# Hybrid attention and retention layer: what goes through which pass of the input projection, how squares and input sums are made, and the order of the work

## The chip, the cores and the metric

The kernel runs on one core of one Trainium2 chip. The metric is the time of one execution on the device in microseconds; lower is better. A profiled execution of the kernel before is at hand: every instruction of the five engines (TensorE = PE, VectorE = DVE, ScalarE = ACT, GpSimd = POOL, SyncE = SP, which issues most transfers) and every transfer, with start and duration.

## What is computed

One decoder layer on 4096 rows of width 1024, float32. An RMS norm is followed by one input projection whose columns feed two groups: eight heads of rotary, dilated window attention and four heads of retention. Both are gated, concatenated, projected back and added to the input; a last RMS norm closes.

```python
def reference(x, norm_gain, w_in, ret_gn_gain, w_out, final_gain):
    for layer in range(DEPTH):
        h = rms_norm(x, norm_gain[layer])
        x = x + hybrid_mixer(h, w_in[layer], ret_gn_gain[layer], w_out[layer])
    return rms_norm(x, final_gain)

def hybrid_mixer(h, w_in, ret_gn_gain, w_out):
    proj = h @ w_in
    qa, ka, va, ga, qr, kr, vr, gr = jnp.split(proj, cuts, axis=-1)
    attn = merge_heads(dilated_attention(qa, ka, va))   # heads split; rotary q, k; branches (128,1), (512,4), (2048,16)
    ret = merge_heads(retention(qr, kr, vr))            # rotated q, k; chunks of 128; group norm
    ret = ret * ret_gn_gain
    mixed = jnp.concatenate([jax.nn.silu(ga) * attn, jax.nn.silu(gr) * ret], axis=-1)
    return mixed @ w_out
```

What matters here is `proj` for the attention's q, k, v and the retention's q, k ("r" below), with the rotation of q, k and r.

## The kernel before

The program has three stages. Stage 1 (`phase1`) makes q, k, r and v and writes them to device memory. Stage 2 (`phase2`) reads them back and computes attention and retention; stage 3 makes the gates and the output projection. Only stage 1 is touched.

**Passes, blocks, steps.** Stage 1 goes twice over the 4096 positions, each time in 8 blocks of 512 (`BLK`), so in 16 blocks `q` = 0 to 15; `q < NBLK` (8) is pass 0. A pass computes two groups of 512 output columns, `bank` 0 and 1. Before, pass 0 made q (bank 0) and k (bank 1), pass 1 made r (bank 0) and v (bank 1). The weights of a pass lie in SBUF; those of pass 1 are made while the last block of pass 0 and the first of pass 1 run.

**Seven products in place of eight.** A block's product of a 2 x 2 arrangement is made with seven smaller products of sums (Strassen's scheme in Winograd's form). The input of a block is split into four tiles of 128 x 1024 elements: `a1`, `a2` are the first and second 256 positions of the upper half of the contraction, `b1`, `b2` those of the lower. P1 takes a1, P2 b1, P3 b2, and P5, P6, P7, P4 take sums of them (`sum_t`, n = 1 to 4, on GpSimd, into tiles `d` of their own). Each product accumulates in one of three kinds of PSUM bank, `x` (3 buffers), `y` (2) or `z` (2), by the table `SUMS`. `snapshot` copies a bank's state to a tile `m` on ScalarE, `join` adds a bank to such a tile on VectorE.

**Precision.** Each factor is split into a high part (ScalarE, `AF.Copy` to the rounded type) and a low part (the rest, on VectorE or GpSimd), and each product is three products of parts: 24 matrix products of 128 x 128 by 256 columns for one product and bank. That is one *step*; a block has `STEPS` = 14 steps, two for each entry of `PRODUCTS`, bank 0 and then bank 1.

**What sets the order.** The order is written by hand and kept on every engine. `at(step, function, ...)` enters work for a step, and the loop at the end of the function goes through the steps, emits the step's product and then what is entered for it. `s` is the first step of a block, so an entry at `s + 11` stands in the block's twelfth step and one at `s + 17` in the fourth step of the next block. On each engine instructions run in this order; SP issues the transfers in this order, and one that has to wait holds back those behind it.

**Around a block.** `load_x` brings the input in two halves of 1 MB. In pass 0 `square` squares it on ScalarE in eight pieces and adds them up on GpSimd; `root` reduces over the partitions with four products, takes the power on GpSimd and forms a diagonal, `along_free` spreads it over the partitions with a product and stores it for pass 1, which loads it in `load_rb`. `load_tables` loads cosines and sines of the block into one buffer `tab`, `scale_tables` multiplies them by the norm's factors on GpSimd. `last_sum` calls `rotate` (six VectorE operations on 512 columns) for q, k and r in two halves of 256 positions each, at steps 11, 13, 15 and 17, and stores them: q and k split into high and low part, r as it is. In pass 1 `store_values` stores v three times in the orders that the three branches want, twelve transfers for each half. Buffers: `rawp` 3 inputs of 1 MB, `dp` 2 sums, `op` 2 for `o` (outputs of `rotate`) and 2 for `hl` (split outputs and v), `mp` 7, one for each tag of `tp`.

**Towards stage 2.** Entries at the end of the last block load stage 2's weights (`w2_load`), the first k (`first_k`), input (`first_chunk`) and the first half of q (`first_q`, two steps before the last product).

Of the kernel before, what the change touches and what calls it, by code (L numbers as in the profile page):

```python
# [8 lines left out]
F32 = mybir.dt.float32  # L9
# [16 lines left out]
D = 1024  # L26
# [92 lines left out]
PRODUCTS = ("P1", "P2", "P6", "P5", "P7", "P3", "P4")  # L119
# [19 lines left out]
def phase1(tc, io, dr, right, ahead):  # L139
# [5 lines left out]
    with ExitStack() as ctx:  # L145
# [33 lines left out]
        def pieces(p, tags, n):  # L179
            def get(dt):  # L180
# [23 lines left out]
                "P1": ("wh0", "q00"),  # L204
                "P2": ("wh1", "h0"),
                "P6": ("q01", "p40"),
                "P7": ("wl0", "wl1"),
                "P3": ("h1", "q10"),
# [3 lines left out]
                "P2": ("wh0", "wl0"),  # L212
                "P6": ("wh1", "wl1"),
                "P5": ("h0", "h1"),
                "P7": ("q00", "q10"),
                "P3": ("q01", "q11"),
# [4 lines left out]
        def load_w(ps, dst, part, k):  # L221

            rows = io["w1"][k * 128 : (k + 1) * 128, :]
            if ps == 0:
                src = rows[:, 0:1024].rearrange("k (u t c) -> k t u c", t=2, c=128)[:, part]
                nc.sync.dma_start(dst.rearrange("k (u c) -> k u c", c=128), src)
            else:
                src = rows[:, 1024:1536].rearrange("k (u t c) -> k t u c", t=2, c=128)[:, part]
                nc.sync.dma_start(dst[:, 0:256].rearrange("k (u c) -> k u c", c=128), src)
                nc.sync.dma_start(dst[:, 256:512], rows[:, 1536 + 256 * part : 1792 + 256 * part])  # L230
# [41 lines left out]
        xraw, xsum, xs = {}, {}, {}  # L272
        NB2 = 2 * NBLK

        def load_x(q, part, one=None):

            b = q % NBLK
            if (q, part) not in xraw:
                xraw[q, part] = rawp.tile([128, 4, BLK], F32, tag="x", name="xt1")
            cols = slice(b * BLK, (b + 1) * BLK)  # L280
            if one is None:
                nc.sync.dma_start(xraw[q, part], by_blocks(io["xT"])[:, 4 * part : 4 * part + 4, cols])
            else:
                k, hs = one
                cols = slice(b * BLK + hs.start, b * BLK + hs.stop)
                nc.sync.dma_start(xraw[q, part][:, k, hs], io["xT"][(4 * part + k) * 128 : (4 * part + k + 1) * 128, cols])

        H1, H2 = slice(0, HALF), slice(HALF, BLK)

        def sum_t(q, n):  # L290
            a, b = xraw[q, 0], xraw[q, 1]
            if n == 4:
                t = xsum[q, 2]
            else:
                t = dp.tile([128, 4, HALF], F32, tag="d", name="d1")
            x, y, o = {
                1: (a[:, :, H2], a[:, :, H1], ALU.subtract),
                2: (xsum.get((q, 1)), b[:, :, H2], ALU.subtract),
                3: (b[:, :, H2], a[:, :, H2], ALU.subtract),
                4: (b[:, :, H1], t, ALU.add),  # L300
            }[n]
            nc.gpsimd.tensor_tensor(t, x, y, o)  # L302
            xsum[q, n] = t

        def source(q, prod):
            a, b = xraw[q, 0], xraw[q, 1]
            if prod == "P1":
                return a[:, :, H1]
            if prod == "P2":
                return b[:, :, H1]  # L310
            if prod == "P3":
                return b[:, :, H2]
            return xsum[q, {"P5": 1, "P6": 2, "P7": 3, "P4": 4}[prod]]

        def split_x(q, prod, engine=None, each=False):
            t = xs[q, prod] = hp.tile([128, 2, 4, HALF], F32R, tag="h", name="h1")
            src = source(q, prod)
            for ks in [slice(k, k + 1) for k in range(4)] if each else [slice(0, 4)]:
                nc.scalar.activation(t[:, 0, ks, :], src[:, ks, :], AF.Copy)  # L319
                (engine or nc.vector).tensor_tensor(t[:, 1, ks, :], src[:, ks, :], f32(t[:, 0, ks, :]), ALU.subtract)  # L320

        sums = {}

        def square(q, j):

            sq = tp.tile([128, BLK], F32, tag="sq" if j else "acc", name="sq1")
            nc.scalar.activation(sq, xraw[q, j // 4][:, j % 4, :], AF.Square)
            if j:
                nc.gpsimd.tensor_tensor(sums[q], sums[q], sq, ALU.add)
            else:  # L330
                sums[q] = sq

        def root(b):

            ss = pss.tile([128, 512], F32, tag="ss", name="ss1")
            acc = sums.pop(b)
            for i in range(4):
                nc.tensor.matmul(
                    ss[:, i : i + 1],
                    acc[:, i * 128 : (i + 1) * 128],  # L340
                    ones[:, 0:1],
                    start=i == 0,
                    stop=i == 3,
                    skip_group_check=True,
                )
            v = sm.tile([128, 4], F32, tag="v", name="v1")
            nc.vector.tensor_scalar(v, ss[:, 0:4], 1.0 / D, NORM_EPS, ALU.mult, ALU.add)
            cols = rs[:, 4 * b : 4 * b + 4]
            nc.gpsimd.tensor_tensor(cols, v, mhalf, ALU.pow)
            diag = tp.tile([128, 4, 128], F32, tag="sq", name="diag1")  # L350
            nc.gpsimd.tensor_tensor(
                diag, ident.unsqueeze(1).broadcast_to([128, 4, 128]), cols.unsqueeze(2).broadcast_to([128, 4, 128]), ALU.mult
            )
            return diag

        def along_free(b, diag):

            ps = pss.tile([128, BLK], F32, tag="ss", name="rb1")
            nc.tensor.matmul(ps, ones, diag.rearrange("p c i -> p (c i)"), start=True, stop=True)
            rb = tp.tile([128, BLK], F32, tag="rb", name="rb1")  # L360
            nc.scalar.activation(rb, ps, AF.Copy)
            nc.sync.dma_start(dr["rs"][b].rearrange("(o i) p -> o (i p)", o=1), rb[0:1, :])
            return rb
# [7 lines left out]
        def load_tables(q):  # L371
            b, n = q % NBLK, "AR"[q // NBLK]
            tab = tabs[q] = tp.tile([128, 2, BLK], F32, tag="tab", name="tab1")
            for i, nm in enumerate((f"cos{n}", f"sin{n}")):
                nc.sync.dma_start(tab[:, i, :], io[nm][:, b * BLK : (b + 1) * BLK].unsqueeze(0).broadcast_to([4, 32, BLK]))

        def scale_tables(q):
            for i in range(2):
                nc.gpsimd.tensor_tensor(tabs[q][:, i, :], tabs[q][:, i, :], rbs[q], ALU.mult)
# [65 lines left out]
        def value_tile(q, half):  # L445
            if (q, half) not in vfs:
                vfs[q, half] = op.tile([128, 2, 512], F32, tag="hl", name="vo1")
            return vfs[q, half]
# [1333 lines left out]
```

## Time and profile before

| | us |
|---|---|
| median of 3 runs | 2683.66 (2680.44 to 2690.35) |
| the profiled execution | 2687.92 |
| its span, first to last instruction | 2685.8 |

| engine | busy us | share of the span |
|---|---|---|
| TensorE, products | 2347.0 | 87% |
| VectorE | 1734.0 | 65% |
| ScalarE | 1117.9 | 42% |
| GpSimd | 991.5 | 37% |

The shares are means over three stages with different limits. In the page's row of TensorE by fortieths of the span (67 us each) the first fifteen, stage 1, hold 3 to 7 tenths, and nearly all later ones 9.

### The profile page before, as it was taken

To read this page: it belongs to the slowest core of one execution; us is meant where nothing else is said; L and a number is where in the kernel's file an instruction comes from. 1 tells how busy PE (TensorE), PEld (TensorE's weight loads), DVE (VectorE), ACT (ScalarE), POOL (GpSimd) and SP (SyncE) were. 2 spreads that over 40 slices of the span, in tenths; PEclk is the share of its full clock that TensorE was granted. 3 is DMA by queue.
4 is the path that set the end of the run, shared out by engine and by line. 5 is a ranking of instruction groups with operands and counts; after the bars stand their busy time and mean duration, and the time that the engine had idled before them with its cause. 6 is when DMAs were issued, how large, how long until landed. Compare 5 with 4: busy or idle time off the path is not lost.

```text
span 2685.8 us, 47219 instructions
## 1 busy us (share of the span) xinstructions
PE 2347.0 (87%) x16872; PEld 2116.3 (79%) x16872; DVE 1734.0 (65%) x4129; ACT 1117.9 (42%) x3039; POOL 991.5 (37%) x860
## 2 busy tenths in 40 slices
PE   3677777667788756999999999999889999999998
PEld 3677777667788754888888888888678999989997
DVE  5676667685434434777878878888676565656563
ACT  3433333342122112666666666666632232323231
POOL 4544554543232333443534435344622121212110
PEclk7888888879888877999999999999999999999999
DMA  4233333533444356586576765855577656566563
GB/s 132 89 110 121 107 102 103 165 122 109 130 134 153 111 161 178 139 183 149 134 182 143 172 156 139 191 125 133 171 180 169 152 154 155 153 154 152 159 141 103
DMA packets 450074, 383.90 MB, mean 143 GB/s; under 512 B 193224, under 2 KB 397128, under 8 KB 444720
## 3 DMA queue, kind: packets, MB, share of 16 engines
q1 hardware_dynamic: 449024, 379.06, 53.6%
q8 instruction: 133, 2.18, 0.3%
q0 software_dynamic: 528, 1.58, 0.2%
q14 instruction: 101, 0.83, 0.1%
q10 hardware_dynamic: 288, 0.26, 0.0%
HBM read 262.15 MB, written 118.64 MB: 142 GB/s over the span
## 4 chain that ended last, share of the span: by engine, by line
PE 57%; DMA 14%; DVE 13%; SPq 4%; issue 4%; ACT 4%; POOL 4%; DVEq 0%; ACTq 0%; POOLq 0%
PE S L987 8%; PE O L1057 6%; PE T L1024 5%; PE po L48 4%; PE po L50 4%; PE po L49 4%; PE g L49 4%; PE g L50 4%; PE g L48 4%; PE x L407 3%; DMA tab<-in_cosR_dram 3%; PE V L48 2%; DMA tab<-in_sinA_dram 2%; PE V L50 2%; DMA dr_v<-vo 2%
## 5 line engine op out<-in xcount | busy, mean ns | idle before, releaser
L1008 DVE CUSTOM_DVE_ANT_0 S<-S,mask 128x256 f32<-128x256 f32 (+1 forms) x768 | 308.4, 402 | 181.9 <-PE S L987 147.8
L1015 ACT ACTIVATE P<-S,nm 128x256 f32<-128x256 f32 (+1 forms) x768 | 337.3, 449 | 50.7 <-DVE nm L1008 47.5
L50 PE MATMUL g<-h,wg 128*128 128x256 f32 x1024 | 290.2, 283 | 0.0
L407 PE MATMUL x<-h,w1q 128*128 128x256 f32 x832 | 181.1, 316 | 68.3 <-ACT m L428 63.2
L1571 POOL TENSOR_TENSOR rs<-v,mhalf 128x1 f32<-128x1 f32 x32 | 17.5, 547 | 551.9 <-DVE v L1569 534.2
L1024 PE MATMUL T<-ident,P 128*128 128x128 f32 x1368 | 214.1, 274 | 0.0
L407 PEld LDWEIGHTS x<-h,w1q 128*128 128x128 f32 x832 | 150.6, 222 | 71.7 <-ACT m L428 65.6
L49 PE MATMUL po<-wo,m 128*128 128x512 f32 x512 | 200.5, 392 | 0.0
L50 PEld LDWEIGHTS g<-h,wg 128*128 128x128 f32 x1024 | 196.6, 192 | 0.0
L1057 PE MATMUL O<-pt,v 128*64 128x128 f32 (+1 forms) x1968 | 196.4, 326 | 0.0
L987 PE MATMUL S<-kk,qc 128*128 128x256 f32 x1024 | 187.1, 306 | 7.7 <-issue 2.8
L755 POOL TENSOR_TENSOR hc<-hr,hc 128x512 fp32r<-128x512 f32 x64 | 85.4, 1335 | 273.5 <-ACT hc L754 187.6
L48 PE MATMUL po<-wohi,m 128*128 128x512 f32 x448 | 178.9, 399 | 7.1 <-ACT m L40 6.7
L987 PEld LDWEIGHTS S<-kk,qc 128*128 128x128 f32 x1024 | 149.5, 190 | 36.5 <-issue 18.6
L50 PE MATMUL po<-wohi,m 128*128 128x512 f32 x448 | 177.4, 397 | 0.2 <-DVE m L41 0.2
L319 ACT ACTIVATE h<-d 128x1024 fp32r<-128x1024 f32 x64 | 67.7, 1058 | 253.6 <-POOL d L302 147.8
L1057 PEld LDWEIGHTS O<-pt,v 128*64 128x64 f32 x1968 | 121.4, 137 | 60.8 <-issue 32.1
L1024 PEld LDWEIGHTS T<-ident,P 128*128 128x128 f32 x1368 | 164.5, 142 | 0.2 <-ACT wg0hi L87 0.2
L1015 ACT ACTIVATION_READ_ACCUMULATOR P<-S,nm 128x1 f32 x768 | 157.4, 205 | 0.0
L407 PE MATMUL x<-h,w1wh 128*128 128x256 f32 x384 | 89.7, 333 | 74.0 <-DVE o L484 60.5
L1510 ACT ACTIVATE e<-g 128x256 f32<-128x256 f32 x128 | 48.2, 379 | 250.9 <-PE g L50 232.1
L320 DVE TENSOR_TENSOR h<-d,h 128x1024 fp32r<-128x1024 f32 x46 | 70.2, 1526 | 125.1 <-ACT h L319 121.8
(273 smaller groups left out, 6966.8 us busy)
## 6 DMA issues: line engine op xcount, KB each, us to landing
hr<-in_xT_dram SPq DMA_DIRECT2D x64, 512.0 KB
q<-dr_q SPq DMA_DIRECT2D x128, 256.0 KB
xt<-in_xT_dram SPq DMA_DIRECT2D x30, 1024.0 KB
wb<-dr_w SPq DMA_DIRECT2D x128, 192.0 KB
o<-dr_o SPq DMA_DIRECT2D x192, 128.0 KB
v<-dr_v SPq DMA_DIRECT2D x94, 256.0 KB
dr_q<-hl SPq DMA_DIRECT2D x64, 256.0 KB
dr_k<-hl SPq DMA_DIRECT2D x64, 256.0 KB
```

The source lines that it names most:

```text
L48: nc.tensor.matmul(out, wh, xh, start=first and i == 0, stop=False)
L49: nc.tensor.matmul(out, wh, xl, start=False, stop=False)
L50: nc.tensor.matmul(out, wl, xh, start=False, stop=last and i == n - 1)
L319: nc.scalar.activation(t[:, 0, ks, :], src[:, ks, :], AF.Copy)
L320: (engine or nc.vector).tensor_tensor(t[:, 1, ks, :], src[:, ks, :], f32(t[:, 0, ks, :]), ALU.subtract)
L407: nc.tensor.matmul(o, l, r, start=first and j == 0, stop=last and j == 2, skip_group_check=True)
L755: nc.gpsimd.tensor_tensor(hc[:, :, 1, :], src, hc[:, :, 0, :].bitcast(F32), ALU.subtract)
L987: nc.tensor.matmul(s[:, j * 256 : (j + 1) * 256], qq[h, t, half][:, off : off + 128] if br == 0 else it["q"][:, t, i, :], rhs, start=(j == ...
L1008: nc.vector.tensor_tensor_reduce(sv, sv, mask[:, it["br"], c0:256], 1.0, BIG, ALU.add, ALU.min, accum_out=nm[:, col : col + 1])
L1015: nc.scalar.activation(it["P", i // 2][:, i % 2, c0:256], sv, AF.Exp, bias=nm[:, col : col + 1], scale=-1.0, accum_out=den[:, col : col + 1])
L1024: nc.tensor.transpose(t[:, j * 128 : (j + 1) * 128], it["P", bank][:, j // 2, j % 2 * 128 : j % 2 * 128 + 128], ident)
L1057: nc.tensor.matmul(o[64 * bank : 64 * bank + 64, c0 : c0 + 128 * m], vt[h, br, idx // 8][:, idx % 8, :], it["pt"][:, a : a + m, :].rearran ...
```

## The change

Nine things are changed in `phase1`, all of them together:

1. Pass 0 makes k (bank 0) and r (bank 1), pass 1 makes q (bank 0) and v (bank 1). So pass 0 rotates and stores k and r, pass 1 rotates and stores q and stores v.
2. The products come in the order P1, P5, P6, P3, P7, P2, P4, with other homes for their weights.
3. The input of a block comes in four tiles of 512 KB (`xq`, 6 buffers), one for each of a1, a2, b1, b2. `sum_t` runs on VectorE and writes over one of these tiles (a1 three times, a2 once); the tiles `d` are gone.
4. All low parts of the input are made on VectorE; high and low parts are entered at steps of their own (`hi_x`, `lo_x`).
5. The squares are summed along the rows of x as it lies in memory: `load_n` brings 128 rows of 1024 (512 KB) into one buffer `xn`, `square` squares them on ScalarE with a sum along the row. GpSimd's sums and the four products in `root` are gone; its diagonal takes the buffer `xn` too.
6. Tables come in halves with a buffer for each (k's or q's rotation, r's; first and second half), entered 8 to 11 steps ahead of their rotation; GpSimd scales cosine and sine of a half in one operation.
7. Rotation, high part, low part and store are entered at steps of their own. r's rotated output, the split outputs and v share 3 buffers `hl`.
8. In `store_values` the eight transfers for branch 1 are issued by GpSimd in place of SP.
9. Weights and squares of block 0, the weights of pass 1 and the loads for stage 2 are entered at other places; `first_q` comes four steps before the end.

```diff
-PRODUCTS = ("P1", "P2", "P6", "P5", "P7", "P3", "P4")
+PRODUCTS = ("P1", "P5", "P6", "P3", "P7", "P2", "P4")
...
-        rawp = pool("p1x", 3)
+        rawp = pool("p1x", 6)
         hp = pool("p1h", 3)
-        dp = pool("p1d", 2)
...
         op = pool("p1o", 2)
+        hlp = pool("p1hl", 3)
...
+        def sum_t(q, n, engine=None):
+
+            a1, a2, b1, b2 = (xq[q, i, j] for i in range(2) for j in range(2))
+            out, x, y, o = {
+                1: (a1, a2, a1, ALU.subtract),
+                2: (a1, a1, b2, ALU.subtract),
+                3: (a2, b2, a2, ALU.subtract),
+                4: (a1, b1, a1, ALU.add),
             }[n]
-            nc.gpsimd.tensor_tensor(t, x, y, o)
-            xsum[q, n] = t
+            (engine or nc.vector).tensor_tensor(out, x, y, o)
...
+        def load_n(q, i):
+            xn[q, i] = tp.tile([128, D], F32, tag="xn", name="xn1")
+            n = 4 * q + i
+            nc.sync.dma_start(xn[q, i], io["x"][n * 128 : (n + 1) * 128, :])
+
+        def square(q, i):
+
+            if i == 0:
+                sums[q] = sm.tile([128, 4], F32, tag="ssq", name="ssq1")
+            t = xn.pop((q, i))
+            nc.scalar.activation(t, t, AF.Square, accum_out=sums[q][:, i : i + 1])
...
+            tab = tabs[q, n, half] = tp.tile([128, 2, HALF], F32, tag=f"tab{n}{half}", name="tab1")
...
-                    nc.sync.dma_start(dr["v"][1, r0 : r0 + 32].rearrange("(a l) e -> l a e", a=4), vf[r:128:4, u, :])
+                    nc.gpsimd.dma_start(dr["v"][1, r0 : r0 + 32].rearrange("(a l) e -> l a e", a=4), vf[r:128:4, u, :])
...
+            if bank:
+                t = hlp.tile([128, 2, BLK], F32, tag="hl", name="or1")
+                o1, o2 = t[:, 0, :], t[:, 1, :]
+            else:
+                o1, o2 = (op.tile([128, BLK], F32, tag="o", name=f"o{i}_1") for i in "12")
...
+                for n, (part, half) in zip((12, 10, 8, 5), ((0, 0), (0, 1), (1, 1), (1, 0))):
+                    at(s - n, load_x, q, part, half)
+                at(s - 4, hi_x, q, "P1")
+                at(s - 3, lo_x, q, "P1")
+                at(s - 3, sum_t, q, 1)
+                at(s - 2, hi_x, q, "P5")
+                at(s, lo_x, q, "P5")
+                at(s, sum_t, q, 2)
+                at(s + 1, hi_x, q, "P6")
+                at(s + 2, lo_x, q, "P6")
+            if one and q:
+
+                a, d = {1: (-3, 2), 2: (-7, 2), 3: (-10, 2)}.get(q, (-14, 3))
+                for i in range(4):
+                    at(s + a + d * i, load_n, q, i)
+                    at(s + a + d * i + d - 1, square, q, i)
...
+            for n, half, a, c in (("A", 1, -1, 3), ("A", 0, 2, 6), ("R", 0, 4, 8), ("R", 1, 6, 10)):
+                if one or n == "A":
+                    if q:
+                        at(s + a, load_table, q, n, half)
+                    at(s + max(c, {0: 10, 1: 8}.get(q, 0)), scale_table, q, n, half)
...
+            at(s + 10, rotate, q, 0, 1)
+            at(s + 12, hi_o, q, 1)
+            at(s + 13, lo_o, q, 1)
+            at(s + 13, rotate, q, 0, 0)
+            at(s + 14, store_o, q, 1)
+            at(s + 16, hi_o, q, 0)
+            at(s + 18, lo_o, q, 0)
+            at(s + 19, store_o, q, 0)
+            if one:
+                at(s + 15, rotate, q, 1, 0)
+                at(s + 17, rotate, q, 1, 1)
+                at(s + 17, store_r, q, 0)
+                at(s + 18, store_r, q, 1)
             else:
+                at(s + 12, store_values, q, 1)
+                at(s + 14, last_v, q)
+                at(s + 15, store_values, q, 0)
```

More of the change, by code (lines that the diff above doesn't have):

```diff
@@ L305, in source @@
[L305 to L331, printed above, removed]
-        def root(b):
[L335 to L345, printed above, removed]
+        def load_x(q, part, half, k=None):
+            c0 = q % NBLK * BLK + half * HALF
+            if (q, part, half) not in xq:
+                xq[q, part, half] = rawp.tile([128, 4, HALF], F32, tag="x", name="xt1")
+            t = xq[q, part, half]
+            if k is None:
+                nc.sync.dma_start(t, by_blocks(io["xT"])[:, 4 * part : 4 * part + 4, c0 : c0 + HALF])
+            else:
+                nc.sync.dma_start(t[:, k, :], io["xT"][(4 * part + k) * 128 : (4 * part + k + 1) * 128, c0 : c0 + HALF])
@@ new lines, in hi_x, with lo_x @@
+        def hi_x(q, prod, ks=slice(0, 4)):
+            if (q, prod) not in xs:
+                xs[q, prod] = hp.tile([128, 2, 4, HALF], F32R, tag="h", name="h1")
+            nc.scalar.activation(xs[q, prod][:, 0, ks, :], xq[(q, *SOURCE[prod])][:, ks, :], AF.Copy)
+        def lo_x(q, prod, ks=slice(0, 4), engine=None):
+            h, src = xs[q, prod], xq[(q, *SOURCE[prod])]
+            (engine or nc.vector).tensor_tensor(h[:, 1, ks, :], src[:, ks, :], f32(h[:, 0, ks, :]), ALU.subtract)
+        sums, xn, diags = {}, {}, {}
@@ new lines, in store_r, with parts_of @@
+        def store_r(q, half):
+            for part, o in enumerate(turned.pop((q, 1, half))):
+                for u in range(2):
+                    nc.sync.dma_start(dr["r"][u, :, part, :, columns(q, half)], o[:, u * HALF : (u + 1) * HALF])
+        hls = {}
+        def parts_of(q, hl, o):
+            if q >= NBLK:
+                return hl[:, 0, :], hl[:, 1, :], o
+            pv = hl.rearrange("p t (c r l) -> p t c l r", c=4, r=16)
+            return pv[:, 0], pv[:, 1], o.rearrange("p (c l r) -> p c l r", c=4, r=16)
@@ new lines, in phase1 @@
+                at(s - 3, sum_t, q, 1)
[9 more added lines that the diff above has]
+                    at(s + a + d * i + d - 1, square, q, i)
+                e = s + a + 4 * d
+                at(e, root, q)
+                at(e + 1, along_free, q)
+                at(e + 1, copy_rb, q)
+            elif not one:
+                at(s - 2, load_rb, q)
@@ L695, in phase1 @@
+        for k in range(4):
+            split_w(0, "P1", Aa, 0, ks=[k])
+            hi_x(0, "P1", slice(k, k + 1))
+            lo_x(0, "P1", slice(k, k + 1))
+            for bank in range(2):
+                product(W[0], 0, "P1", bank, [k])
         sum_t(0, 1)
+        hi_x(0, "P5")
+        lo_x(0, "P5")
         for k in range(4):
```

298 lines of the change are left out of this document (129 added, 169 removed).

## The prediction

> **What bounds the kernel now.** I read the busy time by stage first, with the windows put on whole blocks: four of pass 0, five of pass 1, the gap behind pass 1, and a piece of stage 2.
>
> ```profile
> core 0: us, PE busy (x) PEld busy (x) DVE busy (x) ACT busy (x) POOL busy (x), PEclk, DMA share, GB/s
> 238.90:484.80 245.90, 189.63 (x1386) 185.57 (x1386) 169.38 (x181) 87.16 (x120) 124.08 (x64) 0.86 0.34 112
> 678.70:952.80 274.10, 213.74 (x1683) 212.88 (x1682) 115.41 (x142) 55.26 (x80) 88.10 (x40) 0.87 0.41 130
> 988.30:1036.00 47.70, 13.59 (x46) 9.75 (x46) 16.09 (x32) 0.00 (x0) 13.01 (x13) 0.63 0.62 156
> 1100.00:1300.00 200.00, 199.34 (x1567) 167.46 (x1568) 156.77 (x587) 137.61 (x475) 87.06 (x100) 1.00 0.67 157
> ```
>
> A block of pass 0 takes 245.9/4 = 61.5 us, one of pass 1 274.1/5 = 54.8 us. In both nobody is full: TensorE stands still for a fifth of the time. Stage 2, which the change does not touch, has TensorE full at clock 1.00. So only stage 1 and the gap behind it can give anything. What would TensorE alone need? The timeline of PE tells it:
>
> ```profile
> 6.96 0.58 PE L407 MATMUL x<-h,w1wh 128*128 128x256 f32 x1 [6.96 <-ACT h L687]
> 930.02 3.04 PE L407 MATMUL x<-w1p,h 128*128 128x256 f32 x24
> 932.90 3.03 PE L407 MATMUL x<-h,w1kk 128*128 128x256 f32 x24
> 947.50 5.42 PE L407 MATMUL x<-w1kk,h 128*128 128x256 f32 x24 [11.57 <-DVE o L484]
> 979.41 3.10 PE L407 MATMUL z<-w1q,h 128*128 128x256 f32 x24 [0.76 <-ACT m L426]
> 985.22 3.04 PE L407 MATMUL x<-w1p,h 128*128 128x256 f32 x24
> ```
>
> One step (24 products) starts 932.90 - 930.02 = 2.88 us after the last, so 14 steps are 40.3 us. Behind a long stall the same 24 take 5.42 us, so a long stall costs 2.4 us more than itself; one of 0.76 us does not. The first product starts at 6.96 us, the last ends at 985.22 + 3.04 = 988.26. Who stalls it? The chain of waits, in order of time, one turn of pass 0 and one of pass 1:
>
> ```profile
> 315.92 5.49 PE x L407 x24
> 324.31 9.74 DMA tab<-in_sinA_dram
> 334.12 1.29 POOL tab L379
> 347.00 1.29 POOL sq L329
> 377.58 5.39 PE x L407 x24
> ...
> 802.99 6.56 DMA dr_v<-vo
> 833.24 6.57 DMA dr_r<-o
> 863.93 12.19 DMA tab<-in_cosR_dram
> ...
> 983.68 17.69 DMA tab<-in_sinR_dram
> 1024.88 7.24 DMA q<-dr_q
> ```
>
> Pass 0 is a ring: tables loaded late into their one buffer, scaled by GpSimd, four rotations on VectorE, the squares summed on GpSimd in between. Pass 1 is a ring of transfers: stores of r and v, then the tables behind them in the same queue. At the end stage 2's loads of q stand behind the last rotation and its stores.
>
> **The change, part by part.** The tables get four buffers and are asked for 8 to 11 steps ahead of their rotation; in pass 1 no r is rotated or stored. Both rings are cut. What is late next is each engine's load, from these rows (timelines of VectorE and GpSimd, then groups by tile and, with the mean in ns behind the comma, from the page):
>
> ```profile
> 300.00 1.23 DVE L320 TENSOR_TENSOR h<-d,h 128x1024 fp32r<-128x1024 f32 x1 [0.26 <-ACT h L319]
> 301.14 0.68 DVE L483 TENSOR_TENSOR t<-x,tab 128x512 f32<-128x512 f32 x1
> 301.75 0.68 DVE L484 TENSOR_TENSOR o<-x,tab 128x512 f32<-128x512 f32 x1
> 305.71 2.39 DVE L502 TENSOR_TENSOR hl<-o,hl 128x512 fp32r<-128x512 f32 x2 [0.75 <-ACT hl L501]
> 314.55 4.42 DVE L502 TENSOR_TENSOR hl<-o,hl 128x512 fp32r<-128x512 f32 x2 [0.65 <-ACT hl L501]
> 314.77 3.21 POOL L302 TENSOR_TENSOR d<-xt,xt 128x1024 f32<-128x1024 f32 x1
> L302 POOL TENSOR_TENSOR d<-xt x16: 2337/2619/3402, 24.6 to 933.9; 128x1024 f32<-128x1024 f32 x16
> L379 POOL TENSOR_TENSOR tab<-tab,rb x28: 1277/1288/1781, 147.2 to 932.6; 128x512 f32<-128x512 f32 x28
> L319 ACT ACTIVATE h<-d 128x1024 fp32r<-128x1024 f32 x64 | 67.7, 1058 | 253.6 <-POOL d L302 147.8
> L1015 ACT ACTIVATION_READ_ACCUMULATOR P<-S,nm 128x1 f32 x768 | 157.4, 205 | 0.0
> ```
>
> From start to start VectorE needs 1.15 us for 1024 columns and 0.60 for 512. Two of L502 need 2.39 us, but 4.42 beside GpSimd's sum: the two engines hold each other up.
>
> *VectorE, pass 0:* 7 low parts and now 4 sums of the input at 1.15 (no row shows such a sum on VectorE; it has the low part's shape, and lies between 1.15 and GpSimd's 2.34 to 3.40; I take 1.15, the same engine's row): 12.7. Four rotations of 6 at 0.60: 14.4. Six joins: 3.6. Four low parts of k at 1.2: 4.8. Sum 35.5 us. GpSimd keeps only four table scalings of 1.29 and the roots, 5 to 8 us, so with every collision 41 to 43. *Pass 1:* 12.7, two rotations 7.2, three joins and four low parts of q at 0.60 to 0.65, and eight operations on half as many columns for v, near 8 together: 28 us. *TensorE:* 40.3 plus about 0.7 for the two products that spread the root. *ScalarE* does the squares, 4 of 1024 columns at 1.06 + 0.21 = 1.3 each, in place of 8 of 512; it has half its time free. So engines alone would allow 41 to 43 us in both passes. Three new waits keep them from it.
>
> *Transfers on few engines.* While only tables fly (267), only r (615), and only v (624), the share of the 16 DMA engines (last column but one) is as here, and at the start, when weights and x fly on all:
>
> ```profile
> 267.00:272.00 5.00, 5.00 (x44) 5.00 (x43) 1.92 (x2) 2.89 (x5) 2.59 (x2) 1.00 0.25 91
> 615.00:617.00 2.00, 0.00 (x0) 0.00 (x0) 1.20 (x2) 0.00 (x0) 0.00 (x0) 1.00 0.27 87
> 624.00:629.00 5.00, 5.00 (x40) 5.00 (x39) 2.87 (x5) 1.78 (x3) 3.17 (x1) 0.89 0.50 155
> 4.00:20.00 16.00, 12.80 (x92) 12.51 (x93) 8.52 (x16) 10.03 (x18) 0.00 (x0) 1.00 1.07 296
> L492 SPq DMA_DIRECT2D dr_r<-o x44: 505/531/716, 613.1 to 889.4; - x44
> ```
>
> That is 4, 4 and 8 engines' worth, at 90 and 155 GB/s, against 296. Pass 0 now has 1 MB of tables, 1 MB of r, and 6 MB of x, rows of x and k on all 16. At 90 GB/s the first two hold the four engines 2 MB/90 = 23 us, the rest takes 6 MB/296 = 20 us: 43 us of each block, as much as TensorE. The queue on those four never gets short.
>
> *The second rotation of r.* Its output shares 3 buffers with the two halves of k's split and r's first rotation; all are held until stored. The first can start when the block's last product ends, behind k's rotation and two inputs: it is done some 7 to 8 us into the next block. Its four stores then need 4 x 0.53 us to issue and 6.57 us to land (row 833.24). So the second writes from about 16, and sum, low part and P3 behind it on VectorE come at 16 + 3.0 + 2.3 = 21, where P3 is due at 6 x 2.88 = 17.3. I price this at 4 us a block, plus the slow restart of 0 to 2.4: by the rows above a stall of 0.76 is free, one of 11.57 is not; I take 1.5.
>
> The Trainium skill, "TensorE: Matmul & The Clock Gate", Part 1, says that the clock drops after an idle window of 3.4 us and needs as long to come back. By it a 4 us stall would mostly pay the whole 2.4, 0.9 us a block above my value, 6 us in all.
>
> *Rows of x.* Four loads of 512 KB share one buffer, each square waits for its load on ScalarE, each next load on SP for the square. The nearest row is twice the bytes:
>
> ```profile
> 513.66 5.37 DMA xt<-in_xT_dram
> 1011.04 1.83 POOL L936 DMA_DIRECT2D v<-dr_v x2
> ```
>
> So 4 x (5.4 + 1.3) = 27 us in series if the queue is empty, and with 0.75 MB of tables and r at 90 GB/s ahead of two of them (8 us more each) 43. It fits in a block of 48, barely; I add 1.5 for what slips. Behind a late row wait, on ScalarE, snapshots and splits. Pass 0 so takes 41 + 4 + 1.5 + 1.5 = **48 us a block**, from 42 (nothing waits) to 61.5 (a ring as long as the old one).
>
> *v by GpSimd.* Eight of the twelve stores of a half of v go to GpSimd's queue, at 0.92 us to issue (row 1011.04: two in 1.83), 7.4 us in all, and v's buffer is one of the same three. It is complete some 30 us into the block, landed at 30 + 7.4 + 3 = 41, and VectorE's last join or ScalarE's split waits for it; behind come a rotation and the low part of P5: some 3 to 4 us late. Pass 1: 40.3 + 3.7 = **44 us a block**, from 41 to 52. Taking these issues from SP is worth nothing by itself: SP was only waiting in its own ring.
>
> *Ends.* Block 0: P5 ends only when 4 MB are in (14 us at 296 GB/s), summed and split, and P6's sums follow: 18 us of waits, my estimate. Four rows of x, 27 us in series, fall into five steps, 14.4 us: 12 late. So block 1 starts at 7 + 40 + 18 + 12 = 77 us (66 to 90). At the hand-over VectorE gets 40 splits and sums of weights as before, and has less idle time for them: 20 us. Behind the last product stage 2 waits 44 us, to 1032, for q behind r's last tables, stores and v. Now no table is late and q's first half is asked for four steps before the end; but the masks stand in GpSimd's queue behind 16 stores of v, near 15 to 20 us. I take 25 us saved (10 to 40).
>
> **Sum.** 77 + 7 x 48 + 20 + 8 x 44 = 785 us for the last product, in place of 988: 203 less, and 25 behind it, 228 in all. The profiled execution took 2687.9 us (span 2685.8, 2.1 around it), so 2460; the median of the runs, 2683.7, lies 0.16% below it: **2456 us**.
>
> **Rivals.** *Nothing waits:* GpSimd's collisions are gone and the buffers suffice; blocks of 42 and 41 us, 15 more saved at the end: 2456 - 42 - 24 - 15 = 2375. For it: no engine's load is above 43. Against: four DMA engines loaded to 43 us of 42.
>
> *The new ring in pass 0 is as long as the old:* the change would not do there what it says. 7 x 13.5 = 95 more: 2551. For it: rows of x behind r and tables, 43 us by my count without any slip.
>
> *GpSimd's stores crawl:* if each waits for a VectorE operation of 1.15 us, eight need 16.6 us in place of 7.4, and all of pass 1 waits 8 us a block more: 2456 + 64 = 2520. For it: row 314.55 shows the engines hold each other up. Against: row 1011.04, where two issue in 1.83 us.
> The Trainium skill, "SBUF — State Buffer", "SBUF: two separate sides", describes this trap: transfers from GpSimd's queue starve while VectorE has the shared port. It names VectorE's two-port modes, and no row here shows a store issued beside them.
>
> *Slower than before:* the series of rows of x sets pass 0 alone. To lose 228 us and 13 more over 7 blocks a block must take 48 + 35 = 83 us, so a row must need 83/4 - 1.3 = 19.4 us to land. From there on it is slower; at 20 us, 85 us a block, 2456 + 7 x 37 = 2715. For it: 17.69 us in row 983.68, behind the loads of stage 2's weights and k. Against: no load in the middle of a pass took over 12.19.
>
> **Chances.** Forecast, 2410 to 2500: 0.52. Nothing waits: 0.17. Pass 0's ring: 0.14. GpSimd's stores: 0.12. Slower: 0.03; no change, between these: 0.02. A measurement tells some 0.5%, 13 us, from no change; so faster 0.95, same 0.02, slower 0.03. The range takes in the forecast, the third rival and half of the first two: 2375 to 2550.
>
> **What would show it.** Right: P1 to P1 near 48 us in pass 0 and 44 in pass 1; the chain runs through r's stores, VectorE's second rotation and P3, not through tables; no POOL sum; low parts near 1.2 us throughout; the gap behind the last product near 20 us. Wrong: tables or rows of x in the chain with 10 us or more each, GpSimd's issues well over 1 us, or TensorE without gaps, which would mean that I saw waits that are none.

## The result, and the profile after

| | before | after |
|---|---|---|
| median of 4 runs each, us | 2687.01 (2680.44 to 4439.87) | 2567.9 (2566.95 to 2571.75) |
| ratio | | 0.957, 95% interval 0.954 to 0.959 |
| the profiled execution (span), us | 2687.92 (2685.8) | 2571.75 (2570.0) |

One of the four runs of the kernel before took 4439.87 us and is left out of the ratio. The change makes the kernel 4.3% faster. The forecast was 2456, with a range of 2375 to 2550: the sign was right, the time lies outside the range. Of 228 us forecast to go, 116 went (2683.7 to 2567.9).

The windows of the kernel after, put on whole blocks as before: three blocks of pass 0, five of pass 1, the hand-over (blocks 7 and 8), the stretch from the last product of stage 1 to stage 2's first product S, and the same piece of stage 2. The last three rows are pieces of block 4, used further down.

```profile
core 0: us, PE busy (x) PEld busy (x) DVE busy (x) ACT busy (x) POOL busy (x), PEclk, DMA share, GB/s
268.30:436.50 168.20, 133.93 (x1015) 129.97 (x1014) 118.89 (x139) 57.39 (x78) 25.70 (x18) 0.90 0.47 151
614.60:835.50 220.90, 206.53 (x1683) 205.26 (x1683) 150.11 (x190) 65.71 (x100) 56.35 (x90) 0.98 0.62 185
436.50:570.40 133.90, 95.02 (x674) 93.20 (x673) 102.35 (x125) 47.35 (x68) 33.83 (x26) 0.82 0.48 145
879.90:931.40 51.50, 12.88 (x42) 9.69 (x43) 18.72 (x37) 6.53 (x11) 14.50 (x19) 0.60 0.59 154
1100.00:1300.00 200.00, 199.31 (x1566) 167.67 (x1563) 158.46 (x586) 137.38 (x473) 87.01 (x99) 1.00 0.66 155
...
295.50:299.00 3.50, 3.50 (x16) 3.50 (x17) 3.50 (x4) 0.00 (x0) 0.00 (x0) 0.50 0.29 86
299.00:303.00 4.00, 4.00 (x31) 4.00 (x30) 1.42 (x2) 0.00 (x0) 0.00 (x0) 0.84 0.97 312
303.00:307.00 4.00, 4.00 (x35) 4.00 (x35) 3.09 (x3) 1.06 (x1) 1.29 (x1) 1.00 0.52 173
```

A block of pass 1 takes 220.9/5 = 44.2 us and TensorE is busy for 93% of it; a block of pass 0 takes 168.2/3 = 56.1 us with TensorE at 80%. So the gap is closed in pass 1 and hardly in pass 0, and the hand-over (133.9 us for two blocks) is worse than either. Stage 2's piece is as before.

From the start of each block's first product to the next one's, in us, read off the timeline of PE:

```
block       0    1    2    3    4    5    6    7  |  8    9   10   11   12   13   14   15 | last product ends
before   91.0 62.7 61.6 61.4 61.4 61.6 61.4 71.1  | 71.5 48.5 54.4 55.6 53.7 54.7 55.4 55.4 |  988.3
forecast   70   48   48   48   48   48   48   48  |   44   44   44   44   44   44   44   44 |  785
after    70.6 60.0 75.3 55.8 55.6 56.4 56.2 60.9  | 73.0 44.2 45.4 44.1 43.4 44.3 43.7 44.4 |  879.9
```

The forecast has 20 us more for the hand-over, in no block, and 7 ahead of block 0. After against forecast: blocks 1 and 2 are 12 and 27 late, blocks 3 to 6 together 32, blocks 7 and 8 together 13 + 29 - 20 = 22, the rest of pass 1 1.5: 95 us, all of it in pass 0 and around the hand-over.

Who waits in the three blocks of pass 0? From the waits of the kernel after, 273 to 442 us, grouped (engine and line, what it waited for: us in total, times, longest; PEld is TensorE's load of weights):

```profile
ACT xn L323 <- DMA xn<-in_x_dram: 58.4, 9, 10.8
...
PE z L390 <- DVE h L309: 23.9, 3, 8.8
DVE or L471 <- DMA dr_r<-or: 23.7, 3, 8.7
...
PEld rb L341 <- POOL diag L332: 9.4, 3, 3.7
```

Two waits reach TensorE, once a block each: 8.0 us at P3 (second row), which is the second rotation of r waiting for r's first stores (third row), and 3.1 us ahead of the block's first product, for the diagonal made of the squares (fourth row). The squares themselves wait for rows of x (first row), 19.5 us a block, on ScalarE. The timelines of block 4 show the first wait from end to end, PE first:

```profile
267.77 1.13 PE L341 MATMUL rb<-diag,ones 128*128 128x512 f32 x2 [2.27 <-POOL diag L332]
...
287.56 0.28 PE L390 MATMUL z<-h,w1kk 128*128 128x256 f32 x1
295.47 8.00 PE L390 MATMUL z<-h,w1kk 128*128 128x256 f32 x47 [7.63 <-DVE h L309]
303.31 5.92 PE L390 MATMUL x<-h,w1w 128*128 128x256 f32 x48
```

VectorE, where the last operation of r's first rotation, the second rotation's first two and P3's low part stand:

```profile
278.81 0.68 DVE L475 TENSOR_TENSOR or<-or,m 128x512 f32<-128x512 f32 x1
279.41 1.21 DVE L297 TENSOR_TENSOR xt<-xt,xt 128x1024 f32<-128x1024 f32 x1
...
281.68 0.68 DVE L470 TENSOR_TENSOR t<-m,tab 128x512 f32<-128x512 f32 x1
289.92 0.69 DVE L471 TENSOR_TENSOR or<-m,tab 128x512 f32<-128x512 f32 x1 [7.56 <-DMA dr_r<-or]
...
294.20 1.22 DVE L309 TENSOR_TENSOR h<-xt,h 128x1024 fp32r<-128x1024 f32 x1
```

And SP, which issues the stores and then the rows of x (x4 is four instructions in 4.13 us). The lower rows are block 2 and the end of stage 1; both come back further down:

```profile
278.92 4.13 SPq L484 DMA_DIRECT2D dr_r<-or  x4
283.14 1.23 SPq L316 DMA_DIRECT2D xn<-in_x_dram  x1
...
298.21 4.09 SPq L516 DMA_DIRECT2D dr_k<-hl  x4
...
305.86 1.41 SPq L316 DMA_DIRECT2D xn<-in_x_dram  x1
...
155.72 0.25 SPq L346 DMA_DIRECT2D dr_rs<-rb  x1
...
157.85 16.89 SPq L484 DMA_DIRECT2D dr_r<-or  x8
...
177.94 1.62 SPq L316 DMA_DIRECT2D xn<-in_x_dram  x1
...
879.55 11.63 SPq L900 DMA_DIRECT2D q<-dr_q  x8
892.76 0.63 SPq L440 DMA_DIRECT2D dr_v<-vo  x1
```

The first rotation ends 279.5 - 268.3 = 11.2 us into the block (forecast 7 to 8), its four stores take 4.13 us to issue (2.1) and are landed at 289.9, 10.4 us after the rotation's end; so the second rotation writes at 21.6 us instead of 16, and P3's low part is ready at 27.1.

### The profile page after: what moved, and what is told of

Its sections match the earlier page's. It is cut to its first block, busy times and chain, and to the rows that moved or that the text cites. A ratio compares the mean times of both kernels' runs of the same rounds, so it can differ in the third digit from the quotient of the medians.

```text
span 2570.0 us, 47422 instructions
## 1 busy us (share of the span) xinstructions
PE 2319.0 (90%) x16808; PEld 2086.2 (81%) x16808; DVE 1758.1 (68%) x4221; ACT 1116.3 (43%) x3036; POOL 751.9 (29%) x853
## 5 line engine op out<-in xcount | busy, mean ns | idle before, releaser
L305 ACT ACTIVATE h<-xt 128x1024 fp32r<-128x1024 f32 (+1 forms) x115 | 118.9, 1034 | 225.8 <-DVE xt L297 99.2
L309 DVE TENSOR_TENSOR h<-xt,h 128x1024 fp32r<-128x1024 f32 (+1 forms) x115 | 155.3, 1355 | 52.1 <-ACT h L305 50.4
L362 POOL TENSOR_TENSOR tab<-tab,rb 128x512 f32<-128x512 f32 x48 | 70.6, 1475 | 339.3 <-DMA tab<-in_sinR_dram 155.7
L48 PE MATMUL V<-w2hi,hc 128*128 128x512 f32 x256 | 118.9, 464 | 37.5 <-DVE hc L792 36.7
L49 PE MATMUL g<-h,wg1hi 128*128 128x256 f32 x512 | 145.7, 285 | 1.9 <-DVE h L843 1.8
```

The source lines that it names most:

```text
L48: nc.tensor.matmul(out, wh, xh, start=first and i == 0, stop=False)
L49: nc.tensor.matmul(out, wh, xl, start=False, stop=False)
L305: nc.scalar.activation(xs[q, prod][:, 0, ks, :], xq[(q, *SOURCE[prod])][:, ks, :], AF.Copy)
L309: (engine or nc.vector).tensor_tensor(h[:, 1, ks, :], src[:, ks, :], f32(h[:, 0, ks, :]), ALU.subtract)
L362: nc.gpsimd.tensor_tensor(tabs[q, n, half], tabs[q, n, half], rb, ALU.mult)
```

## The experiments

The time of a kernel spreads by some 0.5%: the four runs of the last one below lie between 2490 and 2503 us. So beside its time, set against the kernel before on the same chip, I give each experiment's block lengths. Where nothing was touched (pass 0 of e4 and e7) their mean repeats to about 1 us; the end of the last product repeats to 4 (e4, changed in its last steps alone). All are edits of the kernel after; e1, e8 and e10 were run 2, 4 and 4 times, the others once.

| | us | ratio to before | last product ends | mean of blocks 3 to 6 |
|---|---|---|---|---|
| after | 2567.9 | 0.957 | 879.9 | 56.0 |
| e1 second rotation of r two steps later | 2535.7 | 0.942 | 844.7 | 52.6 |
| e2 one row load in four | 2559.8 | 0.951 | 866.1 | 55.0 |
| e3 sums by GpSimd | 2590.8 | 0.962 | 902.9 | 56.7 |
| e4 q's load behind v's stores | 2562.8 | 0.952 | 883.7 | 56.8, not touched |
| e5 = e1 + e2 | 2498.6 | 0.927 | 803.5 | 47.1 |
| e6 = e1, diagonal late and in a buffer of its own | 2543.6 | 0.944 | 855.6 | 52.5 |
| e7 v by SP | 2578.6 | 0.957 | 884.5 | 56.5, not touched |
| e8 = e6 + e4 | 2534.8 | 0.941 | 854.1 | 52.7 |
| e9 rows asked for by ScalarE | 2562.0 | 0.954 | 871.6 | 56.2 |
| e10 = e1 + e9 + e4 | 2497.2 | 0.929 | 818.4 | 49.3 |

**The stall at P3.** e1 enters the second rotation of r, and its store, two steps later, so that P3's low part is ahead of it on VectorE.

```diff
-                at(s + 17, rotate, q, 1, 1)
+                at(s + 19, rotate, q, 1, 1)
...
-                at(s + 18, store_r, q, 1)
+                at(s + 20, store_r, q, 1)
```

> r's second rotation and its store stand two steps later (19 and 20 in place of 17 and 18), behind the low parts of P3 and P7 on VectorE; nothing else is changed. Theory A (the wait of that rotation for r's first stores is what stalls P3): the 7.5 to 8.8 us stall before P3 goes and the restart behind it, blocks of pass 0 fall from 56 to 46 to 48 us, the whole by 50 to 75 us, to about 2495 to 2515. Rival B (the rows of x, one after the other through one buffer, set the length of the block): the wait moves to another place, blocks stay at 53 to 56 and the whole falls by less than 20 us. Rival C (four transfer engines are full with tables and r): the same as B, with late tables or late stores in place of rows.

Measured: 0.9415 of before (0.937 to 0.946, two runs against three), 35 us off stage 1. The waits of e1 from 260 to 412 us, three blocks:

```profile
ACT xn L323 <- DMA xn<-in_x_dram: 73.2, 9, 15.6
...
PEld rb L341 <- POOL diag L332: 23.3, 3, 8.1
```

The wait at P3 is out of the list, so the second rotation of r is what stalled P3. But blocks and time miss what theory A gave (46 to 48, 2495 to 2515): of 8 us a block and a restart, only 3.4 came off, since the wait for the diagonal at the block's start has grown from 3.1 to 7.8 us: a wait moved, as in rival B. ScalarE's wait for rows has grown as well, from 58.4 to 73.2. The stall had hidden the wait for the diagonal.

**The rows of x.** e2 loads only the first of a block's four tiles of rows and squares that one four times; it leaves out the other three, so its output is not the layer's.

```diff
         def load_n(q, i):
+            if i:
+                xn[q, i] = xn[q, 0]
+                return
...
-            t = xn.pop((q, i))
+            t = xn[q, i]
```

> Only the first of a block's four loads of rows of x is made and its tile squared four times, so that the norm's factors are not the reference's; transfers fall by 1.5 MB a block of pass 0. Rival B: ScalarE's waits for rows go, the root is early, blocks of pass 0 fall by 8 us or more, the whole by 60 or more. Theory A: the stall at P3 stays at 7 us or more; only the wait for the diagonal, some 3 us a block, goes: 15 to 35 us in all. Rival C: r's stores land sooner since the engines are freer, the stall at P3 falls below 5 us.

Measured: 2559.8 us, 14 us off stage 1: 7 in block 1 (60.0 to 52.8), 4 in block 2 (75.3 to 70.9), and in blocks 3 to 6 about 1 us each, no more than untouched blocks differ. The waits from 260 to 425 us:

```profile
DVE or L474 <- DMA dr_r<-or: 29.3, 3, 10.1
...
PE z L393 <- DVE h L309: 27.1, 3, 9.7
```

Now P3's stall is 9.0 us a block in place of 8.0. And r's stores take no less time with 1.5 MB less in flight (9.8 us of waiting in place of 7.9): that the rows fill the transfer engines and so delay r is ruled out. e5 does both edits, and so leaves out the same rows.

> The later second rotation of r together with one load of rows in four (the tile is squared four times, so the norm's factors are not the reference's). Theory (two waits in series: behind the one for r's stores stands the one for the rows, which shows as TensorE waiting for the diagonal at a block's start, 8 to 9 us in the run with the later rotation): both stalls go, blocks 3 to 6 fall from 52 to 43 to 46 us, the whole to 2490 to 2510. Rival (the wait moves on once more, to tables or stores): blocks stay above 49 us.

Measured: 2498.6 us, 76 us off stage 1, where e1 and e2 alone sum to 35 + 14 = 49. Blocks 3 to 6 take 47.1 us, close to the 48 of the forecast and a little over the 43 to 46 of the theory. So the two waits overlap in the block: while one stays, it covers a large part of what the other costs.

**The diagonal.** e6 asks whether the wait at the block's start needs the rows to come earlier, or only its product to come later: on top of e1, the diagonal gets a buffer of tag `m`, and the product that spreads it comes three steps later.

```diff
-            diags[b] = tp.tile([128, 4, 128], F32, tag="xn", name="diag1")
+            diags[b] = mp.tile([128, 4, 128], F32, tag="m", name="diag1")
...
-                at(e + 1, along_free, q)
-                at(e + 1, copy_rb, q)
+                w = 4 if q > 3 else 1
+                at(e + w, along_free, q)
+                at(e + w, copy_rb, q)
...
-            for n, half, a, c in (("A", 1, -1, 3), ("A", 0, 2, 6), ...
+            for n, half, a, c in (("A", 1, -1, 4), ("A", 0, 2, 6), ...
```

> The later rotation, and with all rows loaded: the diagonal gets a buffer of another kind (a tile m, so that it no longer holds the rows' buffer), and from block 4 on the product that spreads the root and the copy behind it stand three steps later, the first table's scaling one. Theory: TensorE's wait for the diagonal goes though the rows are as late as before: blocks 4 to 7 at 44 to 48 us, the whole at 2505 to 2520. Rival (ScalarE, late by the rows themselves, holds up the snapshots and high parts behind them): blocks stay at 50 to 53 and the whole within 10 us of the run with the later rotation alone.

Measured: 2543.6 us, 8 more than e1, within the rival's 10; stage 1 ends 11 us later than in e1. The wait for the diagonal is gone, and others stand in its place (waits from 260 to 420 us, three blocks):

```profile
ACT xn L323 <- DMA xn<-in_x_dram: 85.2, 9, 15.1
...
PE x L390 <- DVE o L471: 14.3, 3, 4.8
...
PE x L390 <- ACT m L411: 10.7, 3, 3.6
```

4.8 us a block for k's rotation, whose tables need the diagonal's product, and 3.6 for a snapshot on ScalarE. Blocks 4 to 6 take 54.7 us, 2 more than in e1; block 3, whose product was not moved, takes 45.7. Moving the product only moves the wait, as long as the rows are late.

**The place of the request.** In e9 ScalarE asks for the next rows itself, right behind the square that frees the buffer, and not SP, where the request stands behind stores that wait. No byte is saved. The diagonal has a buffer of its own.

```diff
-            nc.sync.dma_start(xn[q, i], io["x"][n * 128 : (n + 1) * 128, :])
+            nc.scalar.dma_start(xn[q, i], io["x"][n * 128 : (n + 1) * 128, :])
...
             nc.scalar.activation(t, t, AF.Square, accum_out=sums[q][:, i : i + 1])
+            if i < 3:
+                load_n(q, i + 1)
...
-            diags[b] = tp.tile([128, 4, 128], F32, tag="xn", name="diag1")
+            diags[b] = mp.tile([128, 4, 128], F32, tag="m", name="diag1")
...
-                    at(s + a + d * i, load_n, q, i)
+                    if i == 0:
+                        at(s + a, load_n, q, 0)
```

> ScalarE itself asks for the next rows of x, right behind the square that frees their buffer, in place of SP, where the request stands behind stores that wait; the diagonal takes a tile m. The second rotation of r stays where the change put it. Theory (two waits, r's stores first): the stall at P3 stays at 7 us or more, only the wait at a block's start goes: blocks 3 to 6 at 52 to 55, the whole 10 to 30 us below the changed kernel, 2540 to 2558. Rival (the rows were the whole cause): blocks below 50.

Measured: 2562.0 us. The stall at P3 stays, as the theory had it, but the blocks are not at 52 to 55 and the whole not below 2558, and the rival's blocks below 50 are far. Only 8 us are off stage 1, with block 1 going from 60.0 to 55.5, block 2 from 75.3 to 67.6, block 0 from 70.6 to 73.2, and blocks 3 to 6 where they were. The waits from 265 to 410 us:

```profile
DVE or L473 <- DMA dr_r<-or: 35.0, 3, 12.0
...
PE z L392 <- DVE h L309: 28.5, 3, 10.1
...
ACT xn L323 <- DMA xn<-in_x_dram: 14.1, 5, 3.8
```

Rows: 14.1 us in place of 58.4, so it was the place of the request that made most of this wait. The diagonal's own buffer did not do it: e6 has that too, and its rows wait 85.2 us. Nor did ScalarE's own queue do much: in blocks 4 to 6 the rows that it waits for are there 5.4 to 7.1 us after their requests, and in the kernel after 3.3 to 8.9. r: 35.0 in place of 23.7, and P3's stall is now 9.5 us. Again one wait took over from the other. e10 has both mended, and q's load moved as in e4 below.

> The same with r's second rotation two steps later and stage 2's q behind v. Theory: rows come early enough that ScalarE no longer waits for them, so both waits of pass 0 are gone with all rows loaded: blocks 3 to 7 at 45 to 49 us, the whole at 2490 to 2510. Rival (it is the bytes of the rows, not where their request stands, that make them late; the run with one load in four took the bytes away): blocks stay at 51 to 54, the whole at 2525 to 2540.

Measured: 2497.2 us (2489.7 to 2503.2, 4 runs), 0.929 of before (0.9255 to 0.932). It beats both kernels and leaves nothing out. Stage 1 ends 61 us earlier than after, where e1 and e9 alone sum to 35 + 8 = 43. Its window, blocks 3 to 6, and its waits from 245 to 395 us:

```profile
241.30:438.60 197.30, 172.09 (x1313) 166.14 (x1312) 156.71 (x183) 79.18 (x106) 42.08 (x25) 0.93 0.56 175
```

```profile
...
ACT xn L323 <- DMA xn<-in_x_dram: 27.6, 9, 5.3
...
PE x L392 <- DVE h L309: 7.0, 3, 3.1
PEld rb L343 <- POOL diag L334: 6.8, 3, 2.3
```

A block is 49.3 us, just over the 45 to 49 expected, with two waits of 2.3 us left for TensorE, and VectorE is busy for 79% of it.

**Sums and v.** e3 gives the sums of the input back to GpSimd, e7 the stores of v for branch 1 back to SP.

```diff
-            (engine or nc.vector).tensor_tensor(out, x, y, o)
+            (engine or nc.gpsimd).tensor_tensor(out, x, y, o)
```

> The sums of the input are made by GpSimd as before the change, in place. Each takes 2.3 to 3.4 us there and holds VectorE up meanwhile. If VectorE's load matters: 4 sums give VectorE 4.6 us a block back, but cost up to 10 us in which the two hold each other up, 16 blocks: 30 to 80 us slower. If the waits for buffers set the time in pass 0 and TensorE in pass 1, within 15 us of the changed kernel.

```diff
-                    nc.gpsimd.dma_start(dr["v"][1, r0 : r0 + 32].rearrange("(a l) e -> l a e", a=4), vf[r:128:4, u, :])
+                    nc.sync.dma_start(dr["v"][1, r0 : r0 + 32].rearrange("(a l) e -> l a e", a=4), vf[r:128:4, u, :])
```

> The eight stores of a half of v that GpSimd issues are issued by SP again. If SP's issues count in pass 1 (0.6 us each, 16 a block, more where they wait): blocks 9 to 15 go from 44 to 48 us or more, the whole 30 us or more slower. If SP has room there: blocks of 43 to 45 us, the whole within 10 us, faster if GpSimd's way lands later than SP's.

Measured: e3 23 us later in stage 1, blocks of pass 1 46.8 us in place of 44.2; e7 4.6 us later, blocks 9 to 15 44.9 us, and by its time, against before on the same chip, no difference. e3's lie between its two expectations. So VectorE as the place of the sums is worth 15 us (by the ratios) to 23 (by stage 1), and the place of v's stores is worth nothing that can be told.

**The gap behind stage 1.** e4 lets stage 2's load of q come two steps later, behind v's stores.

```diff
-        at(s - 4, first_q)
+        at(s - 2, first_q)
```

> Stage 2's first loads of q are asked for two steps later, behind the stores of v's second half. Theory: at the end ScalarE waits 24.7 us for a split buffer held by v, whose stores stand on SP behind these loads. Then the gap between the last product of pass 1 and the first product behind it falls from 36.7 us to under 20, the whole by 12 to 25 us. Rival: the loads of q themselves are what stage 2 waits for, and the whole is the same or slower by 5 to 15 us.

Measured: the gap from the last product to TensorE's next goes from 36.7 to 23.5 us (under 20 was expected), so the order on SP made 13 us of it; the first S comes 38.2 us behind the last product in place of 51.5, the sixteenth 53.0 in place of 68.2. The whole run gains 5 us against the median, 9 against the profiled execution, less than the 12 to 25 expected: the pass ends 4 us later, though nothing was changed ahead of its last steps.

e8 puts e6 and e4 together.

> All three moves together: later second rotation of r, diagonal in its own kind of buffer and spread later, stage 2's q behind v. If they add up: the 32 us of the first, 10 to 25 of the second and 6 of the third below the changed kernel, 2505 to 2520. If the third is lost in the others: 2510 to 2530.

Measured: 2534.8 us (2530.3 to 2540.8, 4 runs), as e1, and outside both ranges. What q's place wins at the end (the sixteenth S 54.9 us behind the last product, 65.3 in e1) the later product of the diagonal loses in stage 1 (854.1 against 844.7).

## Why the prediction was right, and where it was wrong

**What bounds the kernel before, and that both rings go: right.** No table stands between TensorE and its work in the lists above. Tables are still late for GpSimd, but hidden. e5, with 47 us a block, still has this among its waits from 240 to 385 us, three blocks:

```profile
POOL tab L365 <- DMA tab<-in_sinA_dram: 50.0, 7, 8.9
```

**VectorE's and GpSimd's loads: right.** A sum takes 1.21 us on VectorE (row 279.41), where I took 1.15 between bounds of 1.15 and 3.40, the low part 1.22 (row 294.20).

**Pass 1: right, in the number and in the path**, 44.2 us for a forecast of 44. From the timelines of VectorE, ScalarE and TensorE after, at the turn to the block that starts at 747.50:

```profile
736.23 0.88 DVE L422 SCALAR_TENSOR_TENSOR vo<-x,rs_all,m 128x256 f32<-128x256 f32 x2 [2.15 <-PE x L390]
...
750.26 0.63 ACT L500 ACTIVATE hl<-o 128x512 fp32r<-128x512 f32 x1 [9.35 <-DMA dr_q<-hl]
...
752.96 4.43 PE L390 MATMUL x<-w1kk,h 128*128 128x256 f32 x24 [2.43 <-DVE o L471]
```

One half of v is complete at 737.1, 33 us into its block (forecast 30). ScalarE's split of q waits for that buffer; the store named behind its wait is only the one that came last, in two of the five blocks one of v. Behind it comes q's rotation, which frees the bank for P1: there, and not at P5 as I had it, TensorE waits 2.4 us, and its 24 products take 1.4 us more than the 3.03 of an undisturbed step. 40.3 + 2.4 + 1.4 = 44.1. The price of GpSimd's issues was too high, 0.92 us each. The view of tile `dr_v` of after, POOL's issues from 700 to 760 us (ns: least, median, most):

```profile
L447 POOL DMA_DIRECT2D dr_v<-vo x24: 547/547/585, 711.9 to 759.8; - x24
...
DMA to landing us min/median/max: 3.5/6.3/8.7
```

Eight take 8 x 0.547 = 4.4 us where I had 7.4, and land 6.3 us after their issue where I had 3: the two errors cancel. "GpSimd's stores crawl" falls. The trap of the Trainium skill, "SBUF — State Buffer", "SBUF: two separate sides", does not show here: with VectorE busy for 150.11 of 220.9 us (68%), no such issue took over 0.585 us. That section of the Trainium skill ties it to VectorE's two-port modes, and no view here tells whether VectorE was in one.

**Block 0: the number right by luck**, block 1 starts at 77.2 us for 77. TensorE waits 18.9 us in the block (4.7, 10.0, 3.6 and 0.6), near the 18 of my estimate. But the rows of x, for which I had 12 us, keep ScalarE waiting only 3.3; most of the rest is products that run at a lower clock behind these waits: 50.7 us of products where 14 steps are 40.3, at a granted clock of 0.83.

**"The second rotation of r", 4 + 1.5 us: right in place and mechanism, too small.** The stall is 7.6 to 8.8 us, because the first rotation ends 3 us later than I had it and its four stores are landed 10.4 us behind its end, where I had 2.1 + 6.6 = 8.7. The restart that I put at 1.5 is 2.1: the 47 products behind the stall end 8.0 us after their start, the next 48 after 5.9 (rows 295.47 and 303.31). The granted clock is 0.50 up to 299.0, 0.84 on average from there to 303.0, and 1.00 after that; if it has only these two values, it came back at 300.3, 4.8 us behind the start. The Trainium skill, "TensorE: Matmul & The Clock Gate", Part 1, has these two steps, half and full clock, the full one after at least one busy window of some 3.4 us. The 4.8 us agree with that, and the 2.1 us are nearly the whole 2.4 that I had worked out by this rule and not taken.

**"Rows of x", 1.5 us: the step that failed, in mechanism and size.** I had each row landing in 5.4 us, and 8 more for two of them behind tables and r, as bytes in a queue. What made them late was left out of that count. Requests stand on SP behind stores of r and k that wait for VectorE, and the next can't be asked for before the last is squared. Two timelines show it, SP's above (requests at 283.14, directly behind r's four stores, and at 305.86, behind k's) and that of ScalarE after:

```profile
290.78 1.06 ACT L323 ACTIVATE xn<-xn 128x1024 f32<-128x1024 f32 x1 [6.55 <-DMA xn<-in_x_dram]
314.53 1.06 ACT L323 ACTIVATE xn<-xn 128x1024 f32<-128x1024 f32 x1 [9.96 <-DMA xn<-in_x_dram]
...
187.31 1.06 ACT L323 ACTIVATE xn<-xn 128x1024 f32<-128x1024 f32 x1 [26.47 <-DMA xn<-in_x_dram]
```

These two rows were there 7.6 and 8.7 us after their requests, less than the 13.4 that I had allowed; but the second request came 14.0 us after the square that freed its buffer (from 291.8 to 305.9). Their 3 us at the block's start in the kernel after are not their price: that is seen only with r's stall gone, 7.8 us in e1. A block was to be 41 + 4 + 1.5 + 1.5 = 48; in the trace after it is 42.8 + 8.0 + 2.1 + 3.1 = 56.0. I added the two terms; they stand in series in one block, where one hides behind the other, so no single number of the trace after shows the price of either. The Trainium skill, "DMA: Bandwidth & Descriptors", "Issuing engines are not separate DMA queues", says that issuing from several engines saves only the time of the issue. Here, in e9, it saved the wait ahead of it in SP's order: 44 us of ScalarE's waiting for rows in three blocks (58.4 to 14.1), with the same bytes. The measurement decides.

**Blocks 1 and 2: not seen**, 39 us. In my account they are blocks like the others. But while the rows are catching up from the start of the program, their requests fall elsewhere. In block 2 r's first rotation ends at 149.7 us on VectorE, but its stores are asked for at 157.85, since the store of the root's product (155.72), late with the rows, stands ahead of them on SP. SP then stands 16.89 us among eight stores of r, VectorE waits 16.37 us for the first four, and the row at 187.31 keeps ScalarE waiting 26.47 us. So here the late rows delay r, and r the next rows. TensorE itself waits 10.8 us at P3, 6.3 for a snapshot behind the late row on ScalarE, and 5.3 and 2.1 for two diagonals. With the rows asked for by ScalarE and r late, block 1 takes 55.2 in place of 60.0 and block 2 58.2 in place of 75.3 (e10), 22 of the 39 us.

**The hand-over, 20 us: too small**, 42 measured (60.9 + 73.0 in place of 48 + 44). VectorE is busy for 102.35 of the 133.9 us (76%) and TensorE's clock falls to 0.82. In block 7 P3 stalls 15.9 us behind r's second rotation, which waits 15.8 us for r's stores, twice the 8.0 of the blocks before. e1, e5 and e10 bring the two blocks from 133.9 to between 120.3 and 120.8 us, so r's stall makes some 13 of the 22 us too many; the rest I take to be the weights' splits on VectorE, which no run took apart.

**"Ends", 25 us saved: wrong.** The first S comes 51.5 us behind the last product, in place of 42.7. I had q waiting for late tables and for GpSimd's stores, and had not asked what q is now ahead of. Its eight loads hold SP for 11.63 us (row 879.55), the first of v's last stores stands behind them (892.76), v's buffer is one of the three that q's split needs, and ScalarE stands still. VectorE then waits 21.72 us for a split of stage 2's weights that stands behind it on ScalarE. The timeline of ACT and of PE after, and last of PE before:

```profile
906.77 0.63 ACT L500 ACTIVATE hl<-o 128x512 fp32r<-128x512 f32 x1 [24.68 <-DMA rgain<-in_ret_gain_dram]
```

```profile
916.57 0.76 PE L48 MATMUL V<-w2hi,hc 128*128 128x512 f32 x1 [36.70 <-DVE hc L792]
931.40 0.63 PE L1027 MATMUL S<-kk,q 128*128 128x256 f32 x4
```

```profile
1008.54 0.76 PE L48 MATMUL V<-w2hi,hc 128*128 128x512 f32 x1 [20.29 <-DVE hc L752]
```

(The name behind ACT's wait is only the transfer that came last; e4, where that wait falls to 12.99 us, shows that v's stores behind q make a large part of it.) The 9 us lost here are made up by the sixteenth S, which comes 68.2 us behind the last product after and 68.3 before. So of the 25 us nothing came; e4, with the sixteenth S at 53.0, has 15 of them.

**The sum.** Against the forecast span of 2458: 95 us in stage 1 and 25 at its end, less 7 behind the last S (752.9 us from there to the end, 759.5 before; why stays open), make 2571 for 2570.0 measured. Of the 95 us the later rotation of r and the rows' requests on ScalarE take back 61 together (e10): 27 of 32 in blocks 3 to 6, 22 of 39 in blocks 1 and 2, 14 of 22 around the hand-over. Alone they take back 35 (e1) and 8 (e9).

**The rivals.** "Nothing waits" falls. "The new ring in pass 0" came nearest in time, 2551, and had the rows behind r and tables for it; but blocks are 56 and not 61.5, and the reason was the order on SP, not the load of four transfer engines (e2 against e9). "Slower" falls: in blocks 4 to 6 no row kept ScalarE waiting for over 10.8 us, and even the row of block 2 that came 26.47 us late was there 9.4 us after its request (177.94 to 187.31), where the rival needed 19.4.

## What to carry to other kernels

Two waits that fall in the same block are not two terms of a sum: while one stays, it hides the other, and taking away one alone shows a part of its worth (35 and 8 us alone, 61 together). Before a transfer is priced by its bytes, look at what stands ahead of its request on the engine that issues it, and ask for it from the engine whose work frees its buffer. When a load is moved to an earlier place in a queue, name the stores that are now behind it, and who needs their buffers.

## What was not expected of the hardware

- Four stores of one form took SP 4.13 us to issue at 278.92, and four more 2.26 us at 292.57, in one block of after (SP's timeline). I had priced four by the median of one, 0.53 us. The cause stays open.

```profile
292.57 2.26 SPq L484 DMA_DIRECT2D dr_r<-or  x4
```

- A stall of 7.63 us cost 2.1 us more on the 47 products behind it.
- Fewer bytes in flight did not bring r's stores in sooner: with three of four row loads left out (e2), VectorE waited 9.8 us a block for them, against 7.9.
